# A hybrid attention block with PEER experts: matmul tiles side by side, a wider projection, and three more row buffers in place of descriptor space

## The chip, the core and the metric

The kernel runs on one NeuronCore of a Trainium2 chip. The metric is the device time in microseconds (us) of one execution; lower is better. The engines are named as in the profile: PE (TensorE, matmuls), PEld (its weight loads), DVE (VectorE), ACT (ScalarE), POOL (GpSimd), SP (SyncE, which issues most DMAs).

## The reference, cut

One layer on x of 1024 tokens by 1024 columns, fp32:

```python
u = rms_norm(h, norm_mix_w)
proj = u @ w_in                      # z | xBC | dt | dil q | dil k | dil v | mem q | 3 gates
y_ssd = ssd(conv(xbc), dt, z)        # Mamba-2, chunks of 128, grouped RMS norm at the end
for g, (window, d) in enumerate(((128, 1), (512, 4), (2048, 16))):
    o[g], lse[g] = causal_window_attention(q[g], k[g], v[g], d)   # 4 heads of 64 each
y_dil = sum(softmax(lse over g) * o)
y_mem = softmax(qm @ km.T) @ vm      # 4 heads of 192, 256 memory tokens
h = h + (sum(gate_b * (y_b @ w_b))) @ w_out
hn = rms_norm(h, norm_ffn_w)
expert, gate = product_key_top16(hn) # 8 heads x 16 of 16384 experts per token
h = h + sum(gate * gelu(hn . down[expert]) * up[expert])
```

## The kernel before, in words

**Precision.** A weight or activation is split into a high and a low fp32r part (`split`, L243 to 245), and a product is three matmuls (hi hi, hi lo, lo hi). `mm_feat` keeps weights stationary, `mm_tok` keeps tokens stationary. Small products (sums of squares, attention) are plain fp32; one such matmul shows as two records in the trace.

**Stages.** The tokens are done in two halves of 512 (hf 0 and 1). `front(hf)` runs the SSD branch beside the projections, then `attend`: memory attention (`mem_proj`, `mem_units`, two heads at a time), then the dilated groups 1, 2 and 0 (`dil_project` for q, k, v; `dil_units` and `dil_close`, which call `unit` once for 128 tokens), each beside the next one's projection, and the gated branch projections. `close` multiplies by w_out, adds x, norms and parks. `route` finds the top experts. Then half of the tokens get their experts by dense matmuls (`dense`), the other four tiles of 128 tokens (GATHERED) row by row.

**Sums of squares.** `rms_bcast` (L247 ff.) takes eight or two chunks: each is squared on ACT (L253), and a matmul against one column of ones adds it to a row of PSUM. The row is copied (L256), turned by transposes of one partition (`tr`, L176), and goes through `rsqrt` on DVE.

**V of the dilated groups.** `dil_project` multiplies with the tokens stationary. For groups 1 and 2, `picks[g]` takes every fourth token, a strided operand; each group has its own 256 columns of w_in.

**Attention units.** `unit` does the scores of the heads at partitions 0 to 63 into one PSUM tile, then of those at 64 to 127 into another; each is masked and its maximum taken (L705). `mem_units` handles a head of 192 as pieces of 128 and 64 rows (PIECES), one head's scores after the other's. `dil_order` brings states back into natural order by 32-row matmuls, one tile of tokens after the other. `ps()` hands out PSUM tiles from the tags t and s in turn; in the second half, after `sums_begin`, only s.

**Gathers.** `dots` fetches the down row of each of 128 slots of a tile by an indirect DMA on POOL into a rotating buffer `rowd` (L1115), and DVE dots it with the token's own row (L1109), which takes one of the `rowd` buffers. `ups` fetches up rows, four at a time, into `rowu` (L1168; when no dots are left, every second four into `rowd`), and `add` sums four of them on PE by eight matmuls, each on one 32-column tile of the array (L1154). ND_BUFS = 4, NU_BUFS = 6, and ND_ROWS = 3 rows are issued before a dot.

**What sets the order.** The side jobs (routing heads, dots, ups, early gates) are generators, stepped whenever a running estimate of PE's time (`pe_us`, in `cost`) passes their due time; each step adds its pace (D1 to U4 and others). Engines then run their own instructions in order. Dots and adds are pinned to program order. DMAs are issued in order by SP (weights, parking) and POOL (gathers).

## Time and profile before

| what | us |
|---|---|
| three runs | 3992.51, 3989.93, 3985.82; median 3989.93 |
| the profiled execution, its own time | 3986.07 |
| its span, first to last instruction | 3984.2 |
| busy: PE, PEld | 3734.2, 2804.3 |
| busy: DVE, ACT, POOL | 2755.4, 1501.2, 1177.0 |
| mean granted clock of PE | 0.962 of full speed |
| gathered rows (POOL's queue) | 1024 gathers, 536.94 MB |

To read it: a busy share is an average over the span, so the span is cut at the places where the program passes from one stage to the next. An engine's idle time costs something only where that engine, or one that waits for it, ends the stage.

### The profile page before, as it was taken

What the parts mean: (1) busy time and instruction counts of PE and PEld (TensorE: products, weight loads), DVE (VectorE), ACT (ScalarE), POOL (GpSimd) and SP (SyncE); (2) the same over time, 40 slices, a digit from 0 to 9 for tenths busy, and PEclk for the clock granted to TensorE, in tenths of its full rate; (3) what the DMA queues carried; (4) which work ended last, traced back from release to release, by engine and by line L of the source; (5) the groups of instructions that cost most, each with busy time, mean ns of one, the idle gap of its engine ahead of it and who ended that gap; (6) DMA issues with size and microseconds to landing.
All of it is one profiled execution on the core that took longest, in us unless ns stands there. A gap on an engine that the chain in (4) does not pass through costs nothing.

```text
span 3984.2 us, 54131 instructions
## 1 busy us (share of the span) xinstructions
PE 3734.2 (94%) x17838; PEld 2804.3 (70%) x17838; DVE 2755.4 (69%) x7131; ACT 1501.2 (38%) x3326; POOL 1177.0 (30%) x1081
## 2 busy tenths in 40 slices
PE   8989999999998998998889988899999999999997
PEld 5766888877765786676566666677777777777664
DVE  5763454559998768887759998896667666666432
ACT  4553344343543333454543565222222322222221
POOL 0000000000113323334334423344443444444444
PEclk9999999999999988999899999999999999999998
DMA  3233233444456756798789878889988889988888
GB/s 97 75 98 91 76 109 108 135 151 139 144 170 212 236 179 225 257 312 284 267 300 337 294 254 300 305 320 327 326 321 317 295 322 325 329 319 326 320 301 298
DMA packets 460762, 956.29 MB, mean 240 GB/s; under 512 B 46273, under 2 KB 175041, under 8 KB 460481
## 3 DMA queue, kind: packets, MB, share of 16 engines
q0 software_dynamic: 147456, 536.94, 38.2%
q1 hardware_dynamic: 313024, 415.91, 32.0%
q8 instruction: 140, 2.29, 0.2%
q14 instruction: 142, 1.16, 0.1%
HBM read 882.94 MB, written 69.73 MB: 239 GB/s over the span
## 4 chain that ended last, share of the span: by engine, by line
PE 67%; DVE 11%; DMA 11%; issue 7%; POOL 2%; ACT 2%; SPq 0%; POOLq 0%; ACTq 0%; DVEq 0%
PE mm L172 39%; PE s L172 20%; PE up L1154 5%; PE t L172 3%; DVE rowd L1109 2%; DVE wlo L245 2%; DMA rowd<-in_down_dram,ids 2%; DMA w_park<-work 2%; DMA rowd<-in_up_dram,ids 1%; POOL rowd L1115 1%; DMA wraw<-in_up_dram 1%; PE s L176 1%; DMA wraw<-in_downT_dram 1%; DMA slab<-y_park 1%; DMA wbig<-w_park 1%
## 5 line engine op out<-in xcount | busy, mean ns | idle before, releaser
L244 ACT CAST whi<-wraw 128x512 fp32r<-128x512 f32 (+2 forms) x802 | 489.8, 611 | 1285.9 <-PE mm L172 853.2
L1115 POOL DMA_INDIRECT rowd<-in_down_dram,ids x512 | 593.5, 1159 | 1163.1 <-DVE act L1109 736.6
L245 DVE TENSOR_TENSOR wlo<-wraw,whi 128x512 fp32r<-128x512 f32 (+2 forms) x802 | 540.6, 676 | 535.6 <-ACT whi L244 504.7
L172 PE MATMUL mm<-uslab,whi 128*128 128x512 f32 x2240 | 735.7, 407 | 0.2 <-ACT uslab L244 0.2
L172 PE MATMUL mm<-whi,coef 128*128 128x512 f32 x2048 | 675.8, 400 | 18.4 <-DVE acc L1357 14.3
L1168 POOL DMA_INDIRECT rowu<-in_up_dram,ids x448 | 500.8, 1118 | 622.2 <-PE up L1154 505.4
L1109 DVE CUSTOM_DVE_ANT_0 rowd<-rowd,rowd 128x1024 f32<-128x1024 f32 x512 | 616.5, 1217 | 87.1 <-DMA rowd<-in_down_dram,ids 86.2
L172 PE MATMUL s<-uslab,whi 128*128 128x512 f32 (+1 forms) x2080 | 657.0, 397 | 7.4 <-ACT whi L244 3.1
L172 PEld LDWEIGHTS mm<-whi,coef 128*128 128x128 f32 x2048 | 388.6, 190 | 142.7 <-issue 34.8
L172 PEld LDWEIGHTS mm<-uslab,whi 128*128 128x128 f32 x2240 | 420.3, 192 | 93.4 <-issue 11.4
L172 PEld LDWEIGHTS s<-uslab,whi 128*128 128x128 f32 (+1 forms) x2080 | 386.8, 188 | 130.9 <-issue 36.4
L172 PE MATMUL mm<-uslab,wlo 128*128 128x512 f32 x1120 | 451.6, 406 | 10.3 <-DVE wlo L245 10.2
L172 PE MATMUL s<-uslab,wlo 128*128 128x512 f32 (+1 forms) x1040 | 411.5, 396 | 8.3 <-DVE wlo L245 8.1
L172 PE MATMUL mm<-wlo,coef 128*128 128x512 f32 x1024 | 407.4, 398 | 1.8 <-DVE wlo L245 1.8
L245 DVE TENSOR_TENSOR wlo<-coef,whi 128x512 fp32r<-128x512 f32 x200 | 137.7, 689 | 213.6 <-ACT whi L244 213.6
L172 PE MATMUL mm<-slab,whi 128*128 128x512 f32 x768 | 255.9, 411 | 24.2 <-DVE slab L245 8.4
L244 ACT CAST whi<-coef 128x512 fp32r<-128x512 f32 x200 | 124.1, 621 | 390.6 <-PE s L172 323.6
L172 PEld LDWEIGHTS mm<-uslab,wlo 128*128 128x128 f32 x1120 | 214.3, 192 | 62.9 <-DVE wlo L245 14.2
L1154 PE MATMUL up<-rowu,one_col 128*32 128x512 f32 x1792 | 224.7, 611 | 17.6 <-DMA rowu<-in_up_dram,ids 17.6
L527 POOL COPY slab<-halo 128x3 f32<-128x3 f32 x32 | 12.2, 386 | 763.5 <-DVE posf L1002 747.1
L172 PE MATMUL mm<-whi,uslab 128*128 128x512 f32 (+1 forms) x768 | 236.0, 388 | 0.0
L172 PEld LDWEIGHTS s<-uslab,wlo 128*128 128x128 f32 (+1 forms) x1040 | 195.5, 188 | 56.0 <-DVE wlo L245 11.5
(316 smaller groups left out, 5371.7 us busy)
## 6 DMA issues: line engine op xcount, KB each, us to landing
wraw<-in_up_dram SPq DMA_DIRECT2D x256, 256.0 KB, 5.5
coef<-in_downT_dram SPq DMA_DIRECT2D x200, 256.0 KB, 7.2
wraw<-in_w_in_dram SPq DMA_DIRECT2D x152, 256.0 KB, 2.8
wbig<-w_park SPq DMA_DIRECT2D x128, 256.0 KB, 10.5
wraw<-in_w_in_dram SPq DMA_DIRECT2D x160, 128.0 KB, 2.2
slab<-y_park SPq DMA_DIRECT2D x64, 256.0 KB, 3.6
wraw<-in_w_query_dram SPq DMA_DIRECT2D x64, 256.0 KB, 3.6
w_park<-work SPq DMA_DIRECT2D x64, 256.0 KB, 8.1
```

What stands on the lines that cost most here:

```text
L172: return nc.tensor.matmul(o, lhsT, rhs, **kw)
L176: nc.tensor.transpose(o, x, i)
L244: nc.scalar.copy(hi, src)
L245: nc.vector.tensor_tensor(out=lo, in0=src, in1=hi.bitcast(F32), op=ALU.subtract)
L527: nc.gpsimd.tensor_copy(r[:, 0:3], halo[:, f, :])
L1109: pinned(nc.vector.tensor_tensor_reduce(out=r, in0=r, in1=hn, scale=1.0, scalar=0.0, op0=ALU.mult, op1=ALU.add, accum_out=act[:, j:j + 1]))
L1115: nc.gpsimd.indirect_dma_start(out=r, out_offset=None, in_=down_d, in_offset=bass.IndirectOffsetOnAxis(ap=ids[:, j:j + 1], axis=0))
L1154: pinned(nc.tensor.matmul(up[32 * q:32 * q + 32, hh * 512:(hh + 1) * 512], z[:, q, 31 - n:63 - n], four[q][:, hh * 512:(hh + 1) * 512], st ...
L1168: nc.gpsimd.indirect_dma_start(out=r, out_offset=None, in_=up_d, in_offset=bass.IndirectOffsetOnAxis(ap=ids[:, 128 + t:129 + t], axis=0))
```

## The change

1. `rms_bcast` squares four chunks at a time; the four sums go to four column tiles of PE (ones of 32 columns, tile_position (0, 32 q)), so the sum lies in four quarters of the partitions, and fp32 matmuls against a new column of `cst` (C_STRIP, a one at partitions 0, 32, 64, 96) add the quarters and turn the row, in place of the transposes.
2. `dil_project(1)` projects V of groups 1 and 2 together, 512 columns wide; group 2 takes its half from `kv[hf, "v2"]`. Four slabs hold it in place of two, and V is parked by four DMAs of 256 columns in place of two of 512.
3. `unit`, `mem_units` and `dil_order` issue the matmuls of two heads (or two tiles of tokens) in turn, into two PSUM tiles.
4. The program is built with a descriptor space of 4096 bytes for GpSimd's DMAs. ND_BUFS goes from 4 to 5, NU_BUFS from 6 to 8, ND_ROWS from 3 to 4: three more buffers of 4 KB per partition.

Later lines move: L172 becomes L173, L176 L177, L1115 L1138, L1154 L1177, L1168 L1191.

```diff
-ND_BUFS, NU_BUFS = 4, 6
-ND_ROWS = 3
+ND_BUFS, NU_BUFS = 5, 8
+ND_ROWS = 4
...
-        w = ntile * P
+        w, n = ntile * P, len(chunks)
+        rows = 32 * min(n, 4)
         wide = ps(tag)
-        for k, c in enumerate(chunks):
-            s = work(width=w)
-            nc.scalar.activation(out=s, in_=c, func=AF.Square)
-            mm(wide[0:1, 0:w], ones[:, 0:1], s, start=k == 0, stop=k == len(chunks) - 1)
-        s = work(width=w)[0:1, :]
-        nc.scalar.copy(s, wide[0:1, 0:w])
+        for k0 in range(0, n, 4):
+            four = []
+            for c in chunks[k0:k0 + 4]:
+                s = work(width=w)
+                nc.scalar.activation(out=s, in_=c, func=AF.Square)
+                four.append(s)
+            for q, s in enumerate(four):
+                mm(wide[32 * q:32 * q + 32, 0:w], ones[:, 0:32], s, start=k0 == 0, stop=k0 + 4 >= n, tile_position=(0, 32 * q), skip_group_check=True)
+        s = work(width=w)[0:rows, :]
+        nc.scalar.copy(s, wide[0:rows, 0:w])
...
-            tr(ss[:, i:i + 1], s[:, i * P:(i + 1) * P], ident[0:1, 0:1])
+            mm(ss[:, i:i + 1], s[:, i * P:(i + 1) * P], cst[0:rows, C_STRIP:C_STRIP + 1], start=True, stop=True)
...
+        if g == 2:
+            v_of = kv.pop((hf, "v2"))
+        else:
+            vs = [slab() for _ in range(4 if g else 2)]
...
-        yield from mm_tok(w_in, [(OFF_DV + 256 * g, 256)], 8, u, picks[g], NT, take_v)
+            yield from mm_tok(w_in, [(OFF_DV + 256 * g, 512 if g else 256)], 8, u, picks[g], NT, take_v)
...
-        for hp in range(2):
-            sp = ps()
-            rows = slice(64 * hp, 64 * hp + 64)
-            for hh in range(2):
-                for n, (kT, _) in enumerate(blocks):
-                    mm(sp[:, hh * 256 + n * P:hh * 256 + (n + 1) * P], picks[g](qT[hh], i)[rows], kT[hh][rows], start=True, stop=True)
+        sps = [ps(), ps()]
+        for hh in range(2):
+            for n, (kT, _) in enumerate(blocks):
+                for hp in range(2):
+                    rows = slice(64 * hp, 64 * hp + 64)
+                    mm(sps[hp][:, hh * 256 + n * P:hh * 256 + (n + 1) * P], picks[g](qT[hh], i)[rows], kT[hh][rows], start=True, stop=True)
...
-        for n in range(NT):
-            pp = ps()
+        for n0 in (0, 2):
+            pps = [ps(), ps()]
             for r in range(4):
...
+                for n in (n0, n0 + 1):
+                    mm(pps[n - n0][:, 0:264], cst[32 * n:32 * n + 32, C_Q2 + 3 - r:C_Q2 + 3 - r + P], st1[r][32 * n:32 * n + 32, :],
+                       start=r == 0, stop=r == 3, tile_position=(32 * n, 0))
...
+            sps = [ps(), ps()]
+            for i in range(2):
+                for n in range(2):
+                    for hd in range(2):
+                        ch, r0, nr, _ = PIECES[hd][n]
+                        mm(sps[hd][:, i * 256:(i + 1) * 256], qm[ch][r0:r0 + nr, (i0 + i) * P:(i0 + i + 1) * P], kT[ch][r0:r0 + nr, :],
+                           start=n == 0, stop=n == 1)
...
-            for hd in range(2):
-                for ch, r0, nr, f0 in PIECES[hd]:
-                    for mb in range(2):
+            for n, two in ((0, (0,)), (0, (1,)), (1, (0, 1))):
+                for mb in range(2):
+                    for hd in two:
+                        ch, r0, nr, f0 = PIECES[hd][n]
...
-    nc = _bacc.Bacc("TRN2", target_bir_lowering=False, num_devices=1)
+    nc = _bacc.Bacc("TRN2", target_bir_lowering=False, num_devices=1, dynamic_dma_scratch_size=4096)
```

PE, scores of memory attention in the first half. The names are those of the PSUM tile (t or s, one for each of two heads), of the queries and of the keys. Before:

```order
L172 MATMUL t_3134<-slab_2796,slab_2967 128x256
L172 MATMUL t_3134<-slab_2796,slab_2972 128x256
L172 MATMUL t_3134<-slab_2796,slab_2967 128x256
L172 MATMUL t_3134<-slab_2796,slab_2972 128x256
L172 MATMUL s_3143<-slab_2798,slab_2977 128x256
L172 MATMUL s_3143<-slab_2796,slab_2972 128x256
L172 MATMUL s_3143<-slab_2798,slab_2977 128x256
L172 MATMUL s_3143<-slab_2796,slab_2972 128x256
```

With the change:

```order
L173 MATMUL t_3134<-slab_2796,slab_2967 128x256
L173 MATMUL s_3135<-slab_2798,slab_2977 128x256
L173 MATMUL t_3134<-slab_2796,slab_2972 128x256
L173 MATMUL s_3135<-slab_2796,slab_2972 128x256
L173 MATMUL t_3134<-slab_2796,slab_2967 128x256
L173 MATMUL s_3135<-slab_2798,slab_2977 128x256
L173 MATMUL t_3134<-slab_2796,slab_2972 128x256
L173 MATMUL s_3135<-slab_2796,slab_2972 128x256
```

The two 64-row pieces (those on slab_2972) of the two heads now follow one another, where each stood between two 128-row pieces of its own head.

PE, the V projection of group 1 in the first half (mm: the PSUM tiles; whi and wlo: the weight's parts; uslab: the tokens' parts). Before:

```order
L172 MATMUL mm_3591<-whi_3595,uslab_223 128x256
L172 MATMUL mm_3591<-wlo_3596,uslab_223 128x256
L172 MATMUL mm_3591<-whi_3595,uslab_224 128x256
L172 MATMUL mm_3591<-whi_3595,uslab_227 128x256
L172 MATMUL mm_3591<-wlo_3596,uslab_227 128x256
L172 MATMUL mm_3591<-whi_3595,uslab_228 128x256
```

With the change:

```order
L173 MATMUL mm_3593<-whi_3599,uslab_223 128x512
L173 MATMUL mm_3593<-wlo_3600,uslab_223 128x512
L173 MATMUL mm_3593<-whi_3599,uslab_224 128x512
L173 MATMUL mm_3594<-whi_3599,uslab_223 128x512
L173 MATMUL mm_3594<-wlo_3600,uslab_223 128x512
L173 MATMUL mm_3594<-whi_3599,uslab_224 128x512
```

There are 96 of these either way, now 512 wide; the 96 that stood in group 2's projection are gone.

POOL, gathers of up rows near the end (rowu and rowd are the two sets of buffers; a number is one use of a buffer). Before:

```order
L1168 DMA rowu_34845<-in_up_dram,ids_24572 128x1024
L1168 DMA rowd_34793<-in_up_dram,ids_24572 128x1024
L1168 DMA rowd_34795<-in_up_dram,ids_24572 128x1024
L1168 DMA rowd_34823<-in_up_dram,ids_24572 128x1024
L1168 DMA rowd_34825<-in_up_dram,ids_24572 128x1024
L1168 DMA rowu_34865<-in_up_dram,ids_24572 128x1024
```

With the change:

```order
L1191 DMA rowu_34641<-in_up_dram,ids_24369 128x1024
L1191 DMA rowd_34607<-in_up_dram,ids_24369 128x1024
L1191 DMA rowd_34609<-in_up_dram,ids_24369 128x1024
L1191 DMA rowd_34611<-in_up_dram,ids_24369 128x1024
L1191 DMA rowu_34661<-in_up_dram,ids_24369 128x1024
L1191 DMA rowu_34681<-in_up_dram,ids_24369 128x1024
```

With six and four buffers the two sets come in runs of four of `rowd`; with eight and five the runs are of two and three.

## Rows read from the trace of the kernel before

**Rows 1.** The page: busy time and share of the span of each engine, and the chain that ended last, by engine.

```profile
PE 3734.2 (94%) x17838; PEld 2804.3 (70%) x17838; DVE 2755.4 (69%) x7131; ACT 1501.2 (38%) x3326; POOL 1177.0 (30%) x1081
...
PE 67%; DVE 11%; DMA 11%; issue 7%; POOL 2%; ACT 2%; SPq 0%; POOLq 0%; ACTq 0%; DVEq 0%
```

**Rows 2.** The span cut into stages: from and to, length, then busy time and instructions of PE, PEld, DVE, ACT and POOL, the granted clock of PE, DMA share, GB/s.

```profile
0.00:830.00 830.00, 793.87 (x3739) 619.76 (x3740) 446.98 (x1127) 364.48 (x801) 14.06 (x41) 0.99 0.35 100
830.00:1030.00 200.00, 189.59 (x887) 144.99 (x886) 164.22 (x669) 82.50 (x151) 2.49 (x9) 0.97 0.44 136
1030.00:1500.00 470.00, 438.44 (x1981) 338.78 (x1980) 383.23 (x1097) 175.26 (x397) 138.29 (x125) 0.92 0.62 193
1500.00:1970.00 470.00, 417.63 (x2112) 312.81 (x2110) 392.39 (x1047) 230.75 (x699) 178.23 (x155) 0.93 0.83 282
...
2060.00:2600.00 540.00, 474.43 (x2361) 359.33 (x2360) 477.55 (x1595) 231.39 (x529) 196.61 (x159) 0.95 0.87 297
2600.00:3697.00 1097.00, 1093.20 (x5108) 820.45 (x5107) 746.50 (x1339) 318.78 (x537) 488.19 (x438) 1.00 0.89 322
3697.00:3984.20 287.20, 252.81 (x1306) 160.47 (x1304) 97.62 (x174) 54.50 (x92) 129.38 (x130) 0.94 0.84 303
```

**Rows 3.** The V projections of the first half, groups 1 and 0: length, busy time and records of PE's matmuls into mm, clock, DMA share, GB/s.

```profile
403.90:428.20 24.30, 22.76 (x96) 1.00 0.16 44
...
518.60:531.90 13.30, 12.58 (x97) 1.00 0.27 69
```

**Rows 4.** The stretch of group 1 again, for the weight loads (PEld).

```profile
403.90:428.20 24.30, 22.59 (x96) 1.00 0.16 44
```

**Rows 5.** PE in order of time (start, length, line, operation, records; idle time before): an eight-part sum, a two-part one, the four transposes, and an up-sum with what follows it.

```profile
829.12 7.03 PE L172 MATMUL s<-work,ones 128*1 128x512 f32 x16
...
130.84 1.88 PE L172 MATMUL s<-work,ones 128*1 128x512 f32 x4
...
836.81 0.41 PE L176 MATMUL t<-keep,work 1*128 1x1 f32 x4 [0.67 <-ACT work L256]
...
1655.95 1.92 PE L1154 MATMUL up<-rowu,one_col 128*32 128x512 f32 x16
1657.80 0.50 PE L172 MATMUL mm<-uslab,whi 128*128 128x512 f32 x1
```

**Rows 6.** ACT in order of time: squares of an eight-part sum.

```profile
904.95 1.92 ACT L253 ACTIVATE work<-slab 128x512 f32<-128x512 f32 x3 [0.29 <-DMA slab<-in_xT_dram]
```

**Rows 7.** PE in order of time in memory attention: outputs of one pair of blocks, then the scores of the next.

```profile
1335.20 2.08 PE L172 MATMUL t<-work,slab 128*128 128x256 f32 x8
...
1338.27 1.08 PE L172 MATMUL t<-work,slab 128*64 128x256 f32 x4
1339.28 2.58 PE L172 MATMUL t<-slab,slab 128*128 128x256 f32 x8
1341.79 2.58 PE L172 MATMUL s<-slab,slab 128*128 128x256 f32 x8
```

**Rows 8.** PE in order of time, scores of dilated units: first half group 1 (435), first half group 0 (604), second half (1426), and second half paired (1374 to 1376).

```profile
435.16 0.60 PE L172 MATMUL s<-slab,slab 64*128 64x128 f32 x1
435.17 0.60 PE L172 MATMUL t<-slab,slab 64*128 64x128 f32 x1
...
604.17 0.82 PE L172 MATMUL s<-slab,slab 64*128 64x128 f32 x5
...
1426.37 2.23 PE L172 MATMUL t<-slab,slab 64*128 64x128 f32 x8
...
1374.32 0.60 PE L172 MATMUL t<-slab,slab 64*128 64x128 f32 x1 [1.73 <-ACT slab L653]
...
1376.67 0.60 PE L172 MATMUL mm<-whi,uslab 128*128 128x256 f32 x1
```

**Rows 9.** Waits of DVE from 1030 to 2060: what it waited for, total us, times, longest.

```profile
DVE wlo L245 <- ACT whi L244: 67.4, 41, 10.3
DVE rowd L1109 <- DMA rowd<-in_down_dram,ids: 61.9, 43, 5.3
```

**Rows 10.** Waits of POOL in the same stretch.

```profile
POOL rowd L1115 <- DVE act L1109: 367.0, 97, 14.4
```

**Rows 11.** Waits of PE from 3697 to the end.

```profile
PE up L1154 <- DMA rowd<-in_up_dram,ids: 17.6, 7, 4.1
PE up L1154 <- DMA rowu<-in_up_dram,ids: 11.7, 3, 6.2
```

**Rows 12.** PE in order of time: the first and the last of the last four adds.

```profile
3957.28 3.47 PE L1154 MATMUL up<-rowu,one_col 128*32 128x512 f32 x16 [6.16 <-DMA rowu<-in_up_dram,ids]
...
3975.47 3.64 PE L1154 MATMUL up<-rowd,one_col 128*32 128x512 f32 x16 [2.65 <-DMA rowd<-in_up_dram,ids]
```

**Rows 13.** POOL in order of time, the gather ahead of those adds.

```profile
3949.66 0.93 POOL L1168 DMA_INDIRECT rowu<-in_up_dram,ids  x1 [7.08 <-PE up L1154]
```

**Rows 14.** The gathers' lines: duration ns least, median, most; first and last start, us.

```profile
L1115 POOL DMA_INDIRECT rowd<-in_down_dram,ids x512: 932/958/2319, 1057.4 to 3698.5; - x171
L1168 POOL DMA_INDIRECT rowd<-in_up_dram,ids x64: 932/937/1456, 3710.7 to 3969.3; - x64
```

**Rows 15.** DMA issues of the up rows: count, median us from issue to landing.

```profile
rowu<-in_up_dram,ids POOLq DMA_INDIRECT x448, 7.0
```

**Rows 16.** The page's DMA queue of the gathers: packets, MB, share of 16 engines.

```profile
q0 software_dynamic: 147456, 536.94, 38.2%
```

More of the change, by code (lines that the diff above doesn't have):

```diff
@@ L42 @@
 C_LE, C_GT, C_MCUR, C_MPREV, C_M3C, C_M3P, C_Q2 = 0, 128, 256, 384, 512, 640, 768
-C_SEL, C_INV = 900, 924
-N_CST = 932
+C_SEL, C_INV, C_STRIP = 900, 924, 932
+N_CST = 933
 K_ID, K_IOTA, N_KEEP = 0, 128, 256
@@ L71, in shape_constants @@
     c[:, C_INV:C_INV + 8] = np.exp(np.float32(-math.log(500000.0) * (2.0 / 16)) * np.arange(8, dtype=np.float32))
+    c[0:P:32, C_STRIP] = 1.0
     keep = np.zeros((P, N_KEEP), np.float32)
@@ L640, in dil_project, with take_v @@
             nc.vector.tensor_tensor(out=q3[:, :, 0:16], in0=a, in1=b, op=ALU.add)
-        vs = [slab(), slab()]
-        def take_v(n, pst):
-            nc.scalar.copy(vs[n], pst)
-        yield from mm_tok(w_in, [(OFF_DV + 256 * g, 256)], 8, u, picks[g], NT, take_v)
+        if g == 2:
+            v_of = kv.pop((hf, "v2"))
+        else:
+            vs = [slab() for _ in range(4 if g else 2)]
+            def take_v(n, pst):
+                nc.scalar.copy(vs[n], pst)
+            yield from mm_tok(w_in, [(OFF_DV + 256 * g, 512 if g else 256)], 8, u, picks[g], NT, take_v)
+            if g:
+                v_of, kv[hf, "v2"] = [x[:, 0:256] for x in vs], [x[:, 256:512] for x in vs]
+            else:
+                v_of = [vs[i // 2][:, (i % 2) * 256:(i % 2) * 256 + 256] for i in range(NT)]
         qkT = []
@@ L656, in dil_project @@
         for i in range(NT):
-            kv[hf, g, i] = ([picks[g](k, i) for k in qkT[2:4]], vs[i // 2][:, (i % 2) * 256:(i % 2) * 256 + 256])
+            kv[hf, g, i] = ([picks[g](k, i) for k in qkT[2:4]], v_of[i])
         if hf == 0:
             if g:
-                for n, t in enumerate(qkT[2:4] + vs):
+                for n, t in enumerate(qkT[2:4]):
                     nc.sync.dma_start(kv_park[g, :, n, :], t)
+                for i, v in enumerate(v_of):
+                    nc.sync.dma_start(kv_park[g, :, 2 + i // 2, (i % 2) * 256:(i % 2) * 256 + 256], v)
             else:
@@ L763, in dil_order @@
         nat = states()
-        for n in range(NT):
-            pp = ps()
+        for n0 in (0, 2):
+            pps = [ps(), ps()]
             for r in range(4):
-                mm(pp[:, 0:264], cst[32 * n:32 * n + 32, C_Q2 + 3 - r:C_Q2 + 3 - r + P], st1[r][32 * n:32 * n + 32, :],
-                   start=r == 0, stop=r == 3, tile_position=(32 * n, 0))
-            nc.scalar.copy(nat[n], pp[:, 0:264])
+                for n in (n0, n0 + 1):
+                    mm(pps[n - n0][:, 0:264], cst[32 * n:32 * n + 32, C_Q2 + 3 - r:C_Q2 + 3 - r + P], st1[r][32 * n:32 * n + 32, :],
+                       start=r == 0, stop=r == 3, tile_position=(32 * n, 0))
+            for n in (n0, n0 + 1):
+                nc.scalar.copy(nat[n], pps[n - n0][:, 0:264])
         return nat
@@ L873, in mem_units @@
             mx, l = tiny(4), tiny(4)
-            for hd in range(2):
-                sp = ps()
-                for i in range(2):
-                    for n, (ch, r0, nr, _) in enumerate(PIECES[hd]):
-                        mm(sp[:, i * 256:(i + 1) * 256], qm[ch][r0:r0 + nr, (i0 + i) * P:(i0 + i + 1) * P], kT[ch][r0:r0 + nr, :],
-                           start=n == 0, stop=n == 1)
+            sps = [ps(), ps()]
[5 more added lines that the diff above has]
+                           start=n == 0, stop=n == 1)
+            for hd in range(2):
+                sp = sps[hd]
                 m2 = mx[:, 2 * hd:2 * hd + 2]
```

1 line of the change is left out of this document (added).

## The prediction

> **What bounds the kernel now.** The page's shares of busy time come first: PE is busy 94% of the span, and the chain of work that ended last runs through PE for 67% of its length, with DVE and DMA at 11% each [rows 1]. So removed PE work can count, but an average hides the stages, and I cut the span at the program's joints [rows 2]. Subtract each stage's PE time from its length:
>
> - 0 to 830 (first half): 830 - 793.9 leaves 36 us idle, and DVE is busy only 447. PE decides.
> - 830 to 1970 (second half; from 1030 on the first gathered tile's dots run beside it): PE is idle 94 us in 1140, DVE 200. Both are near their limit, at a granted clock of 0.92 to 0.97.
> - 2060 to 2600 (route): DVE's 477.6 exceeds PE's 474.4, and the change edits nothing that runs there.
> - 2600 to 3697 (dense experts): PE 1093.2 of 1097. Nothing that the change removes lies there, so it counts as zero; gathers that come earlier are hidden by the dense matmuls, at a DMA share of 0.89 already, and would cost something only if they delayed the weights of a PE that has no slack to make it up.
> - 3697 to the end (tail): PE is idle 34.4 us.
>
> The sum is made against the profiled execution, 3986.07 us, which lies 3.9 us (0.1%) under the median of 3989.93. A measurement can tell about 0.2%, 8 us, from no change.
>
> **The wide V projection.** Groups 1 and 2 now take 96 matmuls each and half, 256 columns wide, with every fourth token as stationary operand. The trace gives 22.76 us for 96, 0.237 each; natural-order group 0 takes 12.58 for 97, 0.130 [rows 3]. The strided ones are held by their weight load: PEld is busy 22.59 us of group 1's 24.30 [rows 4]. After the change one set of 96 matmuls, 512 wide, does both groups. Dense matmuls, mostly that wide, take 1093.2/5108 = 0.214 [rows 2], less than the strided load, so each should still take about 0.233 to 0.237 and one whole set falls away: 22.4 us per half. Were load and stream fully added (0.235 + 0.214), 96 x (0.474 - 0.449) = 2.4 would remain: the lower bound. I take 22.4, since the row of 0.237 is itself a load with a stream of 256 hidden behind it. Four slabs are held longer and parking takes six transfers in place of four: SP issues two more per group, nobody waits for parking in the views I read, and I count zero.
>
> **Sums of squares in column quarters.** An eight-part sum takes 7.03 us (16 records), a two-part one 1.88 [rows 5], the memory's, half as wide, some 3.5. An edit of the same shape is already in the kernel: the up-sum's 16 records, in four column tiles, take 1.85 us from their start to the next matmul [rows 5], 3.8 times less than 7.03. So an eight-part sum falls to 1.85 and a two-part one, on half of the array, to about 0.98: PE saves 4 x 5.2 + 8 x 0.9 + about 2.5 = 30 us. [...] Against the 30: each of 13 sums ends in transposes of a 1-partition row, 0.41 us for four [rows 5]; as fp32 matmuls of two records each they take some 0.65 more, 8 in all. And where PE waits for the squares ACT decides: 1.92 for three [rows 6], so 5.1 for eight, and such a sum ends only 1 to 2 us earlier. Net 20, about 10 in the first half, which has the memory's sum, and 9 in the second; bounds 8 (ACT decides all eight-part ones) and 22.
>
> **Halves in turn.** In memory attention a pair of tokens' blocks costs 2.5 + 2.5 us for scores and 4.1 for outputs (1335.20 to 1339.28) [rows 7]. Half of the score matmuls use 64 rows, and the outputs at 1338.27 64 columns. Put next to each other they share the array, as the pair at 435.16 and 435.17 does [rows 8]. A score pair falls to about 3.4 where the turns hold, in about four of eight cases by the order: 7; outputs by 1.2 in eight: 9.6. Together 17, 8 and 9 per half; bounds 0 and 23.
> Units of groups 1 and 2 in the first half run in pairs already [rows 8], so nothing. In the second half some do not: at 1426.37 eight records of one bank run alone for 2.23, while the paired unit at 1374.32 has all sixteen done by 1376.67, 2.35 for both banks [rows 8]. That is about 1.6 in each of about six, with the state pairs of dil_order 8 to 10, taken as 8; group 0 in the first half, five records of one bank before the other starts at 604.17 [rows 8], 3.5. Bounds 0 and 16.
> Removed PE time: first half 22.4 + 10 + 8 + 3.5 = 44, second 22.4 + 9 + 9 + 8 = 48.
>
> **What of it reaches the end.** First half: PE decides, 44. Second half: DVE's work fills parts where PE's is taken out, so I count half, 24.
>
> **Three row buffers.** In 1030 to 2060, DVE stands 61.9 us in 43 waits for down rows [rows 9], while POOL stands 367.0 us for a dot that frees a buffer [rows 10]. Three rows rotate beside the token's own; with four each gather starts one dot earlier. POOL's wait for a dot is 367.0/97 = 3.8 us; by that much sooner a gather can start, so a wait of DVE of 1.44 on average (5.3 the longest) should mostly vanish: I take 40 of 61.9. Again half counts, 20, because DVE's idle time is no loss where PE is the later one. Bounds 0 and 62.
> In the tail PE waits 17.6 + 11.7 us for up rows [rows 11]. The last four adds come some 6 us apart, each behind a gather [rows 12], and POOL itself had waited 7.08 for an add before it could issue the first of those [rows 13]. Eight up rows in place of six, and five in place of four, let a whole group of four rows stand ready behind the one being added. 128 gathers must be issued there at 0.93 each [rows 13, 14], 119 us of 259, so issue does not bind. I take 22 of 34; bounds 0 and 34.
>
> Sum: 44 + 24 + 20 + 22 = 110; 3986 - 110 = **3876 us**.
>
> **Rivals.**
> 1. *DVE bounds the second half and the tail keeps its waits.* For: DVE is idle only 78 us of 470 from 1500 on, and its casts wait for ACT 67.4 us [rows 9], which the change does not touch. Against: PE is the longer of the two there. Then only the first half's 44 remain: 3942.
> 2. *All is recovered.* PE is the longer engine in each part of 830 to 1970, so all of 48 and 40 may count, and all 34 of the tail: 44 + 88 + 34 = 166, 3820. Against: what frees PE brings DVE's 392 of 470 to the front.
> 3. *The change does not do what it says*: tiles still run one after another, because banks or the order of issue part them, and the added transposes cost 8. Then V (22 + 11) and the buffers (20 + 22) remain, 75 - 8 = 67: 3919. Against: the pairs that overlap now [rows 8].
> 4. *Slower: a 4 KB descriptor space holds too few gathers*, and POOL must wait until an earlier one has landed. 1024 gathers run from 1057.4 to 3969.3 [rows 14], one per 2.84 us; an up row lands 7.0 us after issue [rows 15]. With k in flight the rate is 7.0/k: k = 3 gives 2.33 and lengthens only the tail (2.33 against 259/128 = 2.02, +40, still faster in all); k = 2 gives 3.5, 3584 us in place of 2912, +672, less the other 88: about 4570. It decides at k of 2 or less. For: with 0.93 to issue and 7.0 to land six or seven can be in flight, and the space shrinks. Against: POOL's waits name dots and adds [rows 10, 13], none a landing, so the old space is not seen to bind. [...]
>
> **Chances.** Forecast 0.50; only the first half 0.21; all recovered 0.14; tiles that do not overlap 0.06; slower 0.06; within 0.2% 0.03 (contention of earlier gathers taking back what PE gains). The range runs from 3815, all recovered and a little of the upper bounds, to 3945, the first half alone; it leaves out the slower case, no change and the far bounds, under 2 in 10. Faster 0.50 + 0.21 + 0.14 + 0.06 = 0.91, same 0.03, slower 0.06.
>
> **What would show it.** In the changed kernel's profile: the end of the first half near 786 in place of 830; V of both groups in one stretch of some 23 us per half and none in group 2's projection; eight-part sums of about 1.9 us where the squares are ready, 5 where not; score pairs of 3.4; DVE's waits for down rows in the second half at about 20 us in place of 62; PE's waits for rows in the tail at about 10. The forecast is wrong if the second half stays as long as before, if PE's busy time falls by less than 60, or if POOL shows waits for landings that were not there.

## The result, and the profile after

The changed kernel takes 3902.4 us (median of 4 runs, 3898.84 to 3910.26) against 3991.22 of the kernel before; the ratio is 0.9777, 95% interval 0.9758 to 0.9795, so it is about 89 us faster. The forecast was 3876 in a range from 3815 to 3945. The profiled execution of the changed kernel was the slowest of its four: 3910.26, 75.8 under the profiled one of before. What follows on places is told from profiles, what follows on sizes from medians. Each ratio below is known to about 0.002, so a difference between two changed kernels is known to some 10 to 12 us.

PE's busy time fell by 65 us from [rows 1], DVE's by 4:

```profile
PE 3669.4 (94%) x17696; PEld 2769.6 (71%) x17696; DVE 2751.6 (70%) x7131; ACT 1499.4 (38%) x3326; POOL 1185.0 (30%) x1081
```

The span cut at about the same joints of the program as in [rows 2] (the columns are the same; a table at the end of the experiments has sharper joints):

```profile
0.00:807.40 807.40, 770.38 (x3670) 603.30 (x3672) 445.57 (x1126) 363.99 (x801) 14.08 (x41) 0.97 0.36 103
807.40:1007.50 200.10, 189.02 (x878) 143.16 (x873) 156.36 (x612) 82.17 (x151) 4.89 (x9) 0.95 0.44 134
1007.50:1454.00 446.50, 414.29 (x1923) 319.30 (x1922) 391.07 (x1159) 176.55 (x399) 151.99 (x128) 0.92 0.66 208
1454.00:1926.50 472.50, 414.77 (x2102) 318.59 (x2101) 390.19 (x1041) 231.55 (x707) 172.65 (x149) 0.90 0.81 276
...
2014.00:2536.00 522.00, 466.10 (x2323) 352.75 (x2322) 474.49 (x1599) 230.57 (x530) 190.77 (x156) 0.95 0.87 302
2536.00:3627.50 1091.50, 1091.50 (x5115) 819.82 (x5114) 747.02 (x1330) 318.74 (x536) 489.21 (x439) 1.00 0.90 324
3627.50:3908.50 281.00, 250.13 (x1321) 161.43 (x1319) 98.02 (x178) 54.26 (x92) 129.50 (x130) 0.95 0.85 311
```

Line by line against [rows 2]: the first half is 23 us shorter where 44 were expected, 807 to 1926 21 shorter (1119 against 1140) where 44 were expected, the route 18 shorter and the dense stage 5.5 where nothing was, and the tail 6 shorter where 22 were. The granted clock is lower than before in the first row, 0.97 against 0.99, and in the fourth, 0.90 against 0.93.

The wide V projection of the first half (PE's matmuls into mm, columns as in [rows 3]) does what was forecast, 96 records of 0.247 for both groups where [rows 3] had 96 of 0.237 for each (other work of PE runs between them, hence the longer stretch):

```profile
400.50:430.00 29.50, 23.70 (x96) 1.00 0.37 102
```

Memory attention in the changed kernel, PE in order of time: the eight records of 64 columns now take 1.08 us where four took that [rows 7], and the score pieces of 64 rows start 0.01 apart. A pair of scores takes 3.28 us, 345.56 to 348.84, where 5.0 stood before and 3.4 was forecast.

```profile
343.51 1.08 PE L173 MATMUL t<-work,slab 128*64 128x256 f32 x8
...
345.56 0.59 PE L173 MATMUL t<-slab,slab 128*128 128x256 f32 x2
345.99 0.59 PE L173 MATMUL s<-slab,slab 128*128 128x256 f32 x2
346.51 0.48 PE L173 MATMUL t<-slab,slab 64*128 64x256 f32 x1
346.52 0.48 PE L173 MATMUL s<-slab,slab 64*128 64x256 f32 x1
...
348.84 0.73 PE L173 MATMUL mm<-uslab,whi 128*128 128x512 f32 x2
```

The sums are another matter. The first half's closing sum (806.67) takes 2.98 against 7.03 [rows 5] where 1.85 was forecast, and the row's turn behind it 1.05 against 0.41. In the second half's input norm (879 to 895) most of the sum's matmuls stand apart: from 886 on each is two records of 1.04 us between other matmuls, so none of the sum's runs beside another:

```profile
806.67 2.98 PE L173 MATMUL s<-work,ones 128*32 128x512 f32 x16
810.32 1.05 PE L173 MATMUL t<-cst,work 128*128 128x1 f32 x8 [0.68 <-ACT work L262]
...
886.17 0.63 PE L173 MATMUL mm<-uslab,whi 128*128 128x512 f32 x2
886.73 1.05 PE L173 MATMUL t<-work,ones 128*32 128x512 f32 x2
887.71 0.51 PE L173 MATMUL mm<-uslab,wlo 128*128 128x512 f32 x1
888.05 0.61 PE L173 MATMUL mm<-uslab,whi 128*128 128x512 f32 x2
888.60 1.04 PE L173 MATMUL t<-work,ones 128*32 128x512 f32 x2
```

PE's busy time in all the sums (112 records, and four of another use of `ones`), before and in the changed kernel, fell by 16 us, where the forecast's "PE saves" had 30:

```profile
0.00:3984.17 3984.17, 57.81 (x116) 0.96 0.71 240
```

```profile
0.00:3908.50 3908.50, 42.16 (x116) 0.96 0.72 245
```

DVE's waits for down rows, over the whole span (what it waits for, us, times, longest), before and with the change:

```profile
DVE rowd L1109 <- DMA rowd<-in_down_dram,ids: 86.2, 62, 5.3
```

```profile
DVE rowd L1132 <- DMA rowd<-in_down_dram,ids: 30.3, 23, 5.9
```

And the tail's waits did not go; they moved. PE's waits from the issue of the last down row (3628.9) to the end, all for one set of buffers now, against 17.6 + 11.7 in [rows 11]:

```profile
PE up L1177 <- DMA rowd<-in_up_dram,ids: 22.5, 4, 11.1
```

### The profile page after: what moved, and what is told of

It is laid out like the page before. It is cut to its first block, busy times and chain, and to the rows that moved or that the text cites. A ratio compares the mean times of both kernels' runs of the same rounds, so it can differ in the third digit from the quotient of the medians.

```text
span 3908.5 us, 53881 instructions
## 1 busy us (share of the span) xinstructions
PE 3669.4 (94%) x17696; PEld 2769.6 (71%) x17696; DVE 2751.6 (70%) x7131; ACT 1499.4 (38%) x3326; POOL 1185.0 (30%) x1081
## 5 line engine op out<-in xcount | busy, mean ns | idle before, releaser
L1138 POOL DMA_INDIRECT rowd<-in_down_dram,ids x512 | 593.3, 1159 | 1115.3 <-DVE act L1132 727.2
L173 PE MATMUL mm<-uslab,whi 128*128 128x512 f32 x2240 | 739.5, 407 | 3.8 <-DVE slab L433 1.5
L1191 POOL DMA_INDIRECT rowu<-in_up_dram,ids x448 | 506.8, 1131 | 618.5 <-PE up L1177 480.6
L173 PE MATMUL mm<-whi,coef 128*128 128x512 f32 x2048 | 671.3, 398 | 5.5 <-DVE acc L1380 4.3
L173 PE MATMUL s<-uslab,whi 128*128 128x512 f32 (+1 forms) x2080 | 658.8, 398 | 10.0 <-ACT whi L245 4.5
L173 PEld LDWEIGHTS mm<-uslab,whi 128*128 128x128 f32 x2240 | 421.0, 192 | 99.2 <-issue 12.0
L173 PEld LDWEIGHTS s<-uslab,whi 128*128 128x128 f32 (+1 forms) x2080 | 388.9, 189 | 130.2 <-issue 33.0
L173 PEld LDWEIGHTS mm<-whi,coef 128*128 128x128 f32 x2048 | 386.2, 189 | 127.4 <-issue 28.9
L173 PE MATMUL mm<-uslab,wlo 128*128 128x512 f32 x1120 | 453.3, 407 | 10.0 <-DVE wlo L246 9.9
L173 PE MATMUL s<-uslab,wlo 128*128 128x512 f32 (+1 forms) x1040 | 413.5, 398 | 16.0 <-DVE wlo L246 15.5
L173 PE MATMUL mm<-wlo,coef 128*128 128x512 f32 x1024 | 405.6, 396 | 2.3 <-DVE wlo L246 2.3
L173 PE MATMUL mm<-slab,whi 128*128 128x512 f32 x768 | 260.0, 418 | 15.4 <-ACT slab L428 5.2
L173 PEld LDWEIGHTS mm<-uslab,wlo 128*128 128x128 f32 x1120 | 214.5, 192 | 64.9 <-DVE wlo L246 14.6
L173 PEld LDWEIGHTS s<-uslab,wlo 128*128 128x128 f32 (+1 forms) x1040 | 196.5, 189 | 64.6 <-DVE wlo L246 18.5
L173 PEld LDWEIGHTS mm<-wlo,coef 128*128 128x128 f32 x1024 | 193.5, 189 | 47.5 <-DVE wlo L246 4.1
L1177 PE MATMUL up<-rowu,one_col 128*32 128x512 f32 x1792 | 217.5, 599 | 0.0
```

The lines of the kernel that those rows point to most:

```text
L173: return nc.tensor.matmul(o, lhsT, rhs, **kw)
L1138: nc.gpsimd.indirect_dma_start(out=r, out_offset=None, in_=down_d, in_offset=bass.IndirectOffsetOnAxis(ap=ids[:, j:j + 1], axis=0))
L1177: pinned(nc.tensor.matmul(up[32 * q:32 * q + 32, hh * 512:(hh + 1) * 512], z[:, q, 31 - n:63 - n], four[q][:, hh * 512:(hh + 1) * 512], st ...
L1191: nc.gpsimd.indirect_dma_start(out=r, out_offset=None, in_=up_d, in_offset=bass.IndirectOffsetOnAxis(ap=ids[:, 128 + t:129 + t], axis=0))
```

## The experiments

Twelve kernels ran, each timed five times or more beside the kernel before. The ratio is to the kernel before.

| run | what it is | median us | ratio, 95% interval |
|---|---|---|---|
| undo_buffers | changed, old buffers and space | 3964.95 | 0.9937, 0.9917 to 0.9957 |
| undo_sums | changed, old sums | 3883.05 | 0.9725, 0.9703 to 0.9748 |
| undo_wide_v | changed, V apart | 3917.15 | 0.9819, 0.9794 to 0.9845 |
| undo_turns | changed, halves one after the other | 3910.41 | 0.9788, 0.9763 to 0.9812 |
| only_buffers | before + buffers and space | 3944.47 | 0.9892, 0.9874 to 0.9909 |
| only_space | before + 4 KB space | 3992.42 | 1.0004, 0.9992 to 1.0015 |
| only_sums | before + new sums | 4004.35 | 1.0031, 1.0018 to 1.0043 |
| sums_last_first | changed, fourth part's matmul first | 3894.31 | 0.9751, 0.9734 to 0.9767 |
| buffers_and_v | before + buffers + wide V | 3906.22 | 0.9780, 0.9762 to 0.9798 |
| old_sums_new_turn | changed, old sums, fp32 turn | 3910.46 | 0.9783, 0.9765 to 0.9801 |
| new_turn_old_estimate | the same, old estimate | 3891.17 | 0.9758, 0.9740 to 0.9777 |
| undo_sums_third | changed, old sums, other order of up buffers | 3865.44 | 0.9680, 0.9657 to 0.9703 |

**undo_buffers.**

```diff
-ND_BUFS, NU_BUFS = 5, 8
-ND_ROWS = 4
+ND_BUFS, NU_BUFS = 4, 6
+ND_ROWS = 3
-    nc = _bacc.Bacc(..., dynamic_dma_scratch_size=4096)
+    nc = _bacc.Bacc(...)
```

> The changed kernel with the old buffers (4, 6 and 3 rows) and the old descriptor space; the other three parts stay. Theory (the buffers shorten DVE's waits for down rows, and these reach PE through whatever is queued behind a dot on DVE): DVE's waits for down rows go from 30 us back to about 85, PE's idle time in the route and dense stages rises by about 20, and the time is about 3922 against 3902. Rival (DVE's waits end where PE is the later engine, so they are free): the waits come back but the time stays within 8 us of 3902. As forecast (20 in the second half and 22 in the tail): about 3944.

3965: the buffers are worth 62 us in the changed kernel, more than any of the expectations. By the profiles, which lie 48 us apart, 18 of it is in the second half, 15 in the route and 13 in the tail. DVE's waits for down rows come back, as the theory had it (whole span):

```profile
DVE rowd L1132 <- DMA rowd<-in_down_dram,ids: 78.6, 65, 4.8
```

**undo_sums.** The function `rms_bcast` of the kernel before in the changed one.

```diff
-            for q, s in enumerate(four):
-                mm(wide[32 * q:32 * q + 32, 0:w], ones[:, 0:32], s, ..., tile_position=(0, 32 * q), ...)
+            mm(wide[0:1, 0:w], ones[:, 0:1], s, start=k == 0, stop=k == len(chunks) - 1)
...
-            mm(ss[:, i:i + 1], s[:, i * P:(i + 1) * P], cst[0:rows, C_STRIP:C_STRIP + 1], start=True, stop=True)
+            tr(ss[:, i:i + 1], s[:, i * P:(i + 1) * P], ident[0:1, 0:1])
```

> The changed kernel with the old sums of squares (one column of ones, transposes of the row). Theory (the column tiles share the array only where the four matmuls of a group stand next to each other on PE; in the second half's input norm and in the two-part sums they mostly don't, and the extra fp32 matmuls for the row cost 8): 5 to 12 us slower, about 3910. As forecast (20 us of PE time, about 14 of it on the path): about 3917. Rival (what PE saves it loses again, since ACT's squares end these sums): within 5 us of 3902.

3883, 19 us faster than the changed kernel. Each of the first two expectations has the wrong sign, and it is outside the rival's 5 us too: the new sums cost. In the first half, where the forecast had 10 us for them, the two kernels take the same time, 816.6 and 816.8; the loss is in the second half, 1114.4 against 1149.9.

**undo_wide_v.**

```diff
-            yield from mm_tok(w_in, [(OFF_DV + 256 * g, 512 if g else 256)], 8, u, picks[g], NT, take_v)
+        yield from mm_tok(w_in, [(OFF_DV + 256 * g, 256)], 8, u, picks[g], NT, take_v)
```

> The changed kernel with V of groups 1 and 2 projected apart again, 256 wide. Theory (192 strided matmuls at 0.237 in place of 96 at about 0.27 per half, PE decides in both halves): 20 + 18 us slower, about 3940. Forecast's step (22 in the first half, half of 22 in the second): about 3935. Rival (DVE bounds the second half): 20 us, 3922.

3917, 15 us slower (17 by the ratios): less than any expectation, and nearest the rival, which had 20. The first half is 15 longer (831.5 against 816.8), the second the same (1150.8 against 1149.9); so far this spoke for a second half that PE's work does not decide.

**undo_turns.** `unit`, `mem_units` and `dil_order` as before.

```diff
-        for hh in range(2):
-            for n, (kT, _) in enumerate(blocks):
-                for hp in range(2):
+        for hp in range(2):
+            for hh in range(2):
+                for n, (kT, _) in enumerate(blocks):
```

> The changed kernel with unit, mem_units and dil_order as before: the heads' matmuls one half after the other. Theory (8 us of memory attention in each half, 5 of units in the second, 2 to 3 of the state order in each, all PE time): 20 to 26 us slower, about 3925. Forecast's step: 12 in the first half and half of 17 in the second, about 3922. [...]

3910, 8 us slower (4 by the ratios): not clear of no change, and under both expectations. The clock is 0.963 to 0.967 in these five runs against 0.958 to 0.963 in the changed kernel's four. But the turns alone also separate two kernels with the old sums, buffers_and_v and undo_sums below: there they gain 23 us and the clock does not fall (0.963 to 0.966 without them, 0.965 to 0.968 with them), so it is not shown that the turns lower it. Four parts taken out one by one add to 62 - 19 + 15 + 8 = 66, not 89. Four such differences together leave some 25 us open, so the sum alone does not show that the parts depend on each other; each had to be put in as well.

**only_buffers.**

```diff
-ND_BUFS, NU_BUFS = 4, 6
-ND_ROWS = 3
+ND_BUFS, NU_BUFS = 5, 8
+ND_ROWS = 4
-    nc = _bacc.Bacc(...)
+    nc = _bacc.Bacc(..., dynamic_dma_scratch_size=4096)
```

> The kernel before with only the fourth part: 4 KB of descriptor space and 5, 8 and 4 row buffers. Taking this part out of the changed kernel cost 62 us. Theory (the worth of the buffers is their own: DVE, which runs its work in order, no longer stands in front of a dot with casts and masks behind it, PE waits less and its clock falls less often): 45 to 62 us faster than before, about 3935; DVE's waits for down rows near 30 us against 86. Rival (the buffers are worth that much only once PE's own work is shorter): 20 us or less, about 3972.

3944, 49 us by medians, 43 by the ratio: the buffers' worth is their own. DVE's waits for down rows over the span:

```profile
DVE rowd L1109 <- DMA rowd<-in_down_dram,ids: 27.2, 20, 4.9
```

By stages (joints below) the second half is 25 us shorter, the route 5, the dense stage 5, and what follows the last down row 10; the two fives are hardly more than one profile and the next differ by.

**only_space.**

```diff
-    nc = _bacc.Bacc(...)
+    nc = _bacc.Bacc(..., dynamic_dma_scratch_size=4096)
```

> The kernel before with 4 KB of descriptor space and nothing else; the freed 12 KB stay unused. Theory (the space is not what gathers wait for, at most six or seven are in flight): within 8 us of the kernel before, about 3991, with the same gather issues of 0.93 us and landings near 7. Rival (the smaller space holds gathers up and the added buffers outweigh it): 10 us or more slower, and POOL's gathers wait for landings.

No change. POOL waits for what it waited for before (over the whole span, for dots 747.1 us in 204 waits against 736.6 in 201, for adds 496.7 in 95 against 505.4 in 98), and the up rows land in the same time as in [rows 15]:

```profile
rowu<-in_up_dram,ids POOLq DMA_INDIRECT x448, 7.0
```

**only_sums.** `rms_bcast` of the changed kernel and its C_STRIP column in the kernel before.

```diff
-            mm(wide[0:1, 0:w], ones[:, 0:1], s, start=k == 0, stop=k == len(chunks) - 1)
+            for q, s in enumerate(four):
+                mm(wide[32 * q:32 * q + 32, 0:w], ones[:, 0:32], s, ..., tile_position=(0, 32 * q), ...)
...
-            tr(ss[:, i:i + 1], s[:, i * P:(i + 1) * P], ident[0:1, 0:1])
+            mm(ss[:, i:i + 1], s[:, i * P:(i + 1) * P], cst[0:rows, C_STRIP:C_STRIP + 1], start=True, stop=True)
```

> The kernel before with only the first part, the sums of squares in column quarters. Taking this part out of the changed kernel gained 19 us. Theory A (the new form costs by itself: in the second half its matmuls stand apart on PE, 0.976 each against 0.86 side by side with nothing, the row's fp32 matmuls add 8, and PE's waits lower its clock): 8 to 20 us slower than before, about 4004. Theory B (by itself it is worth the little that PE's time in the first half shows, and the 19 us came from the order in which the side jobs then fall): within 8 us of before, or a little faster. Forecast's step: 14 faster, 3977.

4004, 11 to 12 us slower: the time that theory A had, but not all its reasons. PE's time in the sums falls here as well, from 57.81 by 15 us, more than the 8 that the row's matmuls add:

```profile
0.00:4012.37 4012.37, 43.19 (x116) 0.96 0.70 238
```

So the new form does not cost by its own time on PE. What is left is the clock (0.957 against 0.962 over the profiled runs) and the order, for the new turn also changes what the running estimate is charged; this run cannot part them, and new_turn_old_estimate below shows the order's share in the changed kernel. The first half gains 2.5 us, the second loses 17, and the rest some 14 (in a profiled run of 4014.17, 10 over its median).

**sums_last_first.**

```diff
-            for q, s in enumerate(four):
+            for q in [len(four) - 1, *range(len(four) - 1)]:
+                s = four[q]
                 mm(wide[32 * q:32 * q + 32, 0:w], ones[:, 0:32], s, ...)
```

> The changed kernel; in the sums of squares the matmul of the fourth square is issued first, so that the four matmuls of a group wait once and then stand next to each other. Theory A (what costs is that they stand apart): in the second half's input norm a group of four then takes about 1 us in place of 0.976 four times, and the time falls by 5 to 10 us, about 3895. Theory B (order of the side jobs): anything within 12 us of 3902, with no relation to the sums' own time on PE.

3894, 8 us by medians, 10 by the ratios, which is just at the edge of the noise: the time fits theory A at its upper end, and theory B's 12 us as well. The rows speak for A: in the second half's input norm the matmuls of a group now stand together, four in 1.06 us at a clock of 1.00 (the first eight records took 1.76 at a clock of 0.57), and PE's time in all the sums falls from 42.16 to 24.40, 33 under the kernel before, as the forecast had it for sums that share the array:

```profile
878.49 1.76 PE L173 MATMUL t<-work,ones 128*32 128x512 f32 x8 [4.04 <-ACT work L257]
...
883.12 1.06 PE L173 MATMUL t<-work,ones 128*32 128x512 f32 x8
```

```profile
0.00:3895.19 3895.19, 24.40 (x116) 0.96 0.72 246
```

**buffers_and_v.** The kernel before with the buffers, the space and the wide V.

```diff
-ND_BUFS, NU_BUFS = 4, 6
+ND_BUFS, NU_BUFS = 5, 8
...
-        yield from mm_tok(w_in, [(OFF_DV + 256 * g, 256)], 8, u, picks[g], NT, take_v)
+            yield from mm_tok(w_in, [(OFF_DV + 256 * g, 512 if g else 256)], 8, u, picks[g], NT, take_v)
```

> The kernel before with the buffers and the wide V projection, with neither the new sums nor the halves in turn. It stands between the buffers alone (3944 against 3993) and the changed kernel with the old sums (3883). Theory A (V is worth its PE time, 18 in the first half and about as much in the second; the turns are worth theirs, 20 to 25): about 3906. Theory B (in the second half what V frees is taken by the gathers and DVE, as taking V out of the changed kernel cost only 15): about 3926, and then the turns are worth 43.

3906, theory A's number: without the new sums V is worth 38 by medians (45 by the ratios; by the stages 16 in the first half and 27 in the second) and the turns 23 (22). That it came out to the microsecond is luck, for the halves are 16 and 27 where the theory had 18 each. The second half does follow PE's work here, by more than the 22 us that V takes off PE in it.

**old_sums_new_turn.**

```diff
-            tr(ss[:, i:i + 1], s[:, i * P:(i + 1) * P], ident[0:1, 0:1])
+            mm(ss[:, i:i + 1], s[:, i * P:(i + 1) * P], cst[0:1, C_STRIP:C_STRIP + 1], start=True, stop=True)
```

(against undo_sums)

> The changed kernel with the old sums of squares on PE (one column of ones), but the row turned by fp32 matmuls of one partition in place of the transposes. It lies between the old sums (3883) and the changed kernel (3902). Theory A (the turn is 8 us of PE time in all, the tiles that stand apart are the rest): about 3889. Rival 1 (the turn is the whole cost, for it stands at the end of a chain that PE waits for): about 3902. Rival 2 (the cost is in the tiles alone): 3883.

3910: rival 1's time. Fifty small matmuls in place of fifty transposes cost 27 us by medians, 23 by the ratios, though PE's time for the turns themselves grew by about 4 us in each half (in the first, with 26 of the fifty, PE is busy 780.6 against 776.4 in undo_sums; for the second that is an estimate from the first).

**new_turn_old_estimate.**

```diff
-            mm(ss[:, i:i + 1], s[:, i * P:(i + 1) * P], cst[0:1, C_STRIP:C_STRIP + 1], start=True, stop=True)
+            cost(ss[:, i:i + 1], 2); nc.tensor.matmul(ss[:, i:i + 1], s[:, i * P:(i + 1) * P], cst[0:1, C_STRIP:C_STRIP + 1], start=True, stop=True)
```

> As old_sums_new_turn (3910): old sums, the row turned by fp32 matmuls; but the running estimate of PE's time is charged what the transposes were charged, 0.053 us in place of 0.107 for each. All engines then hold the same order as in the kernel with the old sums and the old turn (3883), but for the turn's matmuls themselves. Theory A (the 27 us between these two came from where the side jobs fall once the estimate has moved, by 2.7 us in all, and from the clock that goes with it): 3883 plus some 4 to 8 us of PE time, about 3889. Theory B (the turn itself costs, for the chain behind it waits): about 3910.

3891: theory A. This kernel and old_sums_new_turn hold the same instructions and differ in their order alone, from the second half on; and DVE, ACT, POOL and SP hold the order that they have in undo_sums. The matmuls themselves cost 8 (13 by the ratios); the other 19 (10 by the ratios, at the edge of the noise) came from where the side jobs fell. The second half as one row, first with the new estimate, then with the old one (columns as in [rows 2]):

```profile
819.65:1974.34 1154.69, 1052.59 (x5029) 802.78 (x5029) 959.70 (x2847) 507.16 (x1302) 325.03 (x294) 0.91 0.68 222
```

```profile
820.48:1939.81 1119.33, 1027.46 (x5025) 786.66 (x5025) 957.59 (x2845) 507.27 (x1293) 328.97 (x295) 0.93 0.69 229
```

The work is the same but the second half 35 us longer, at a clock of 0.91 against 0.93; the route gives 9 of them back. (The profiled run of old_sums_new_turn was its slowest, 8 over the median; the other's was 2 over.) Over the whole profiled runs the granted clock is 0.956 and 0.963; if it is at either 1.00 or 0.50, the two values read at the end of this document, that is by estimate 345 us (2 x 0.044 x 3916) at 0.50 against 288.

**undo_sums_third.**

```diff
-            tag = "rowd" if not dots_left and n % 2 else "rowu"
+            tag = "rowd" if not dots_left and n % 3 == 2 else "rowu"
```

(against undo_sums)

> The changed kernel with the old sums of squares, and the last tile's up rows go to the buffers in the order rowu, rowu, rowd (two groups fit in rowu's eight, one in rowd's five) in place of rowu, rowd in turn. Theory (in the tail PE waits 26 us for rowd gathers because rowd holds one group, and its next gather waits for that group's add; with every third group there, three groups are in flight): PE's waits after the dots fall by 10 to 20, about 3868 against 3883. Rival (the place of the adds in PE's order and the pace of the side job set the tail): within 5 us of 3883.

3865, 18 us faster: the theory, a little more than it had. By the profiles 11 of it lie behind the last down row and 7 in the route, which comes before anything that this edit changes and so is not its doing. PE's waits for up rows from the last down row to the end, in undo_sums and here ("issue": nothing that the profile shows released it), fell by 13:

```profile
PE up L1172 <- DMA rowd<-in_up_dram,ids: 26.5, 6, 10.6
```

```profile
PE up L1172 <- issue: 9.1, 2, 7.4
PE up L1172 <- DMA rowu<-in_up_dram,ids: 4.1, 2, 3.2
```

This is the best version: 127 us under the kernel before, and 37 under the changed one.

The stages of the profiles behind these readings, in us. The joints are issues of DMAs that all kernels have: the first parking of the first half's normed tokens, the ninth of its residuals (the second half's first), the first block of the dense weights, the last down row, the end. The instructions of before and only_space stand in the same order, so their rows show what one profile and the next differ by: up to 3 us in a stage. (The 7 in the route of undo_sums and undo_sums_third are of that kind too.)

| kernel | first half | second half | route | dense | after the last down row |
|---|---|---|---|---|---|
| before | 841.7 | 1179.8 | 594.1 | 1082.8 | 285.7 |
| only_space | 844.8 | 1183.0 | 593.9 | 1079.4 | 286.7 |
| only_buffers | 845.0 | 1154.6 | 589.4 | 1077.4 | 276.0 |
| buffers_and_v | 829.1 | 1127.9 | 586.7 | 1078.2 | 281.4 |
| undo_sums | 816.6 | 1114.4 | 594.6 | 1076.9 | 279.2 |
| new_turn_old_estimate | 820.5 | 1119.3 | 593.2 | 1078.7 | 279.5 |
| old_sums_new_turn | 819.6 | 1154.7 | 583.8 | 1077.7 | 280.1 |
| after | 816.8 | 1149.9 | 584.8 | 1077.5 | 279.6 |
| undo_sums_third | 816.9 | 1113.5 | 587.9 | 1077.5 | 267.8 |

## Why the prediction was right in its total, and wrong in a step

Built up part by part, by medians: buffers 49, V 38, turns 23, sums minus 19, together 91; by the ratios 43, 45, 22 and minus 21, together 89. The prediction's terms are 42 + 34 + 20 + 14 = 110. That the total came so near is partly luck: the other three parts gave 14 us more than forecast, against the sums' miss of 33 to 35, and by place the route and the dense stage gave 24 where nothing was forecast. Of the signs that it named, V's stretch (23.70), the score pairs (3.28) and PE's busy time (65 less, where under 60 would have refuted it) came; the end of the first half (807 where 786 was named), the eight-part sums (2.98 and more where 1.9 was), DVE's waits (30 where 20 was) and the tail's (22.5 where 10 was) did not, or not in full.

- **V: right.** 33.6 forecast (22.4 and half of 22.4), 38 to 45 measured. The assumption that the strided weight load and the 512-wide stream run beside each other held: 0.247 in the row above, where one after the other they would take 0.449. Only the halves were off: by the stages 16 in the first, where not all of PE's 22.4 reached the end, and 27 in the second, where all of it counted, not half. Taken out of the changed kernel V is worth 15 to 17, all in the first half.
- **Halves in turn: right in size.** 20 forecast (11.5 and half of 17), 23 measured where the sums are old, 12.5 in the first half and 13.5 in the second by the stages; only 4 to 8 in the changed kernel, not clear of noise. The rows of memory attention show the pairs.
- **Buffers: right in total, wrong in place.** 42 forecast, 43 to 49 measured alone, 62 in the changed kernel (no run says why there more). The second half took 25 of it rather than 20. The tail was mis-sized: 22 forecast, 10 found in only_buffers, and the time from the last dense matmul to the end did not move at all (37.0 us before and after, by the length of that stretch in either profile). The step that failed is that eight and five rows "let a whole group of four rows stand ready". They do for rowu, which holds two groups, but the groups alternate, and rowd's five hold one group and a row. Its next group waits for its own add, as the end of the changed kernel shows, PE first and then POOL:

```profile
3888.24 3.64 PE L1177 MATMUL up<-rowd,one_col 128*32 128x512 f32 x16 [11.07 <-DMA rowd<-in_up_dram,ids]
3891.63 2.28 PE L1177 MATMUL up<-rowu,one_col 128*32 128x512 f32 x16
3900.04 3.64 PE L1177 MATMUL up<-rowd,one_col 128*32 128x512 f32 x16 [6.13 <-DMA rowd<-in_up_dram,ids]
```

```profile
3892.10 0.94 POOL L1191 DMA_INDIRECT rowd<-in_up_dram,ids  x1 [8.45 <-PE up L1177]
```

  With rowd taking every third group what follows the last down row is 267.8 long, 11 less than in undo_sums and 18 less than before, which is most of the 22 that the forecast's term asked for.
- **Sums: the step that failed.** 14 us of gain were forecast on the path, and they cost 11 to 12 alone and 19 in the changed kernel. First, "PE saves" 30 us was mis-sized: 16 were saved. The price of 1.85 us was read from the up-sum, whose 16 records stand together (its matmul for the last row is the first to be issued); the sums' matmuls wait for one square after another and other work gets between them. With the wait moved to the front PE saves 33, and the time falls by 8 to 10. Second, the turn's 8 us were rightly priced (8 to 13 measured), so the column tiles had only some 8 us of PE's time left to gain; old_sums_new_turn and the changed kernel, which differ in the tiles and the order that goes with them, lie 8 us apart by medians and 2 by the ratios. Third, and not in the prediction at all, that is at nothing without a reason: the new turn also charges the running estimate more, 2.7 us in all by 50 x 0.053, and the side jobs fall elsewhere from there on. That alone made 10 to 19 us, and it shows in the second half. The three add to the loss of 19 to 21: 8 or 13 for the turn's matmuls, 19 or 10 for the order, less 8 or 2 for the tiles.
- **Rivals.** Only the first half (3942): refuted, the second half is 30 us shorter by the table, and V alone gave 27 there with the old sums; but its other part, that the tail keeps its waits, came near (22.5 of 29.3 us). All recovered (3820): not reached, though undo_sums_third with the same PE work less the sums comes to 3865. No side by side (3919): refuted for attention by the rows above; for the sum of the second half's input norm it is what happened, with another price. The small descriptor space (4570): refuted by only_space, ratio 0.9992 to 1.0015.

What stays open: why the side jobs' new places cost what they cost. One pair of runs moves them and nothing else (old_sums_new_turn and new_turn_old_estimate), and there the clock is lower and PE is busy longer with the same work; but which job in which place does it, and whether another small shift would gain instead, is not known. Since each part of the change shifts the order, the 15 and 8 us found by taking V and turns out may hold such a share too.

## What to carry to other kernels

An operation is priced from a row with the same neighbours as well as the same shape: column tiles gained here only where their matmuls stood next to each other (1.06 us for four, against 1.04 for one alone), which one arranges by issuing first the matmul whose operand comes last. Where a running cost estimate places side work, a change of what is charged is a change of the order, so keep the charge fixed while the operation is tested, and put parts in one by one as well as taking them out. The two kinds of buffer that are used in turn waited here on the shallower one: 22.5 us of PE's waits behind the last down row were for `rowd`, none for `rowu`.

## What the hardware showed that was not expected

The granted clock fell with PE fully busy. In the changed kernel's first half it is 1.00 from 478 to 485.9 and 0.50 in the next 6.8 us; PE has no idle time in either:

```profile
485.90:492.70 6.80, 6.80 (x26) 5.32 (x24) 1.92 (x14) 2.95 (x12) 0.00 (x0) 0.50 0.00 0
478.00:485.90 7.90, 7.90 (x35) 5.78 (x33) 1.88 (x11) 4.65 (x15) 0.00 (x0) 1.00 0.43 135
```

What PE did just before does not tell why. In undo_sums PE has the same instructions in the same order there, 0.54 us later, and the clock stays at 1.00. Score matmuls of 64 rows and transposes, first in the changed kernel, then in undo_sums, and the clock of undo_sums from 470 to 492:

```profile
483.30 0.83 PE L173 MATMUL t<-slab,slab 64*128 64x128 f32 x2
484.06 0.33 PE L177 MATMUL s<-keep,work 128*128 128x128 f32 x1
484.32 0.82 PE L173 MATMUL s<-slab,slab 64*128 64x128 f32 x2
```

```profile
483.84 0.83 PE L173 MATMUL t<-slab,slab 64*128 64x128 f32 x2
484.60 0.33 PE L177 MATMUL s<-keep,work 128*128 128x128 f32 x1
484.86 0.83 PE L173 MATMUL s<-slab,slab 64*128 64x128 f32 x2
```

```profile
470.00:492.00 22.00, 21.99 (x110) 16.73 (x109) 13.10 (x59) 9.92 (x31) 0.00 (x0) 1.00 0.28 84
```

So the order of PE's work is not shown to be the cause, and the cause stays open.

In four of the kernels the mean clock of the profiled run goes with the time: 0.958 at 3908.5 us of span (changed), 0.963 at 3891.3 (new_turn_old_estimate), 0.965 at 3881.7 (undo_sums) and 0.969 at 3863.7 (undo_sums_third). It does not in all: undo_turns has 0.966 at 3908.6 and undo_wide_v 0.967 at 3916.3. So the clock alone does not set the time. Lower clock came with PE's waits in several places, as in the tail's 0.94 in [rows 2], where PE is idle for 12% of the length, against 1.00 in the dense stage, where it is idle for 0.3%, but the stretch above has it without a wait.
